# One decoder layer on one core: the sample softmax's last group in smaller pieces, prompt attention begun on half the tokens, three mixers moved behind the last attention unit

## The chip, the cores and the metric

The kernel runs on one core of a Trainium2 chip. The metric is the device time in microseconds (us) of one execution, the median over runs. The core has a matrix engine (PE, with its own queue of weight loads, PEld), a vector engine (DVE), a scalar engine (ACT), a general engine (POOL) and a queue that issues DMAs (SP). Each engine runs its own instructions in order and waits for the others by semaphores.

## The reference

One layer of a decoder for a prompt of 1024 tokens and a sample group of 8 x 4 tokens, model width 1024. The part that the change touches is the attention half:

```python
u, v, cq, ckv, kpe = split_in(rms_norm(xp, g_mix[l]) @ w_in[l])
a_out, _ = chunk_gmlp(u, v, w_s[l], b_s[l], ln_v_g[l], ln_v_b[l])
ckv_n = rms_norm(ckv, g_kv_a[l])
q = mla_queries(cq, pos_p, g_q_a[l], w_uq[l], g_qk_q[l])
k, vv = mla_keys_values(ckv_n, kpe, pos_p, w_uk[l], w_uv[l], g_qk_k[l])
b_out = mla_prompt_attend(q, k, vv)
xp = xp + merge_out(a_out, b_out, g_out_a[l], g_out_b[l], w_o[l])
```

There are 8 heads; q and k have 64 columns without and 32 with rotation, and are normalised per head and token; attention is causal. merge_out normalises both halves per token and multiplies by one matrix. The sample tokens do the same, except that each of the 8 sequences attends to 32 pages of 128 cached tokens (latents of 256, from which k is made per head) and to itself. Behind that come an attention to 256 memory tokens and a gated feed-forward with a convolution of width 3, which the change does not touch.

## The kernel before

A float32 product is three matmuls of rounded halves (`mm3`, L185): high by high, low by high, high by low. A tensor's split into halves is a cast on ACT (L191) and a difference on DVE or POOL (L192).

**Start of prompt attention** (`phase2a`, from L600). Tokens come in tiles of 128, in groups of two tiles: four groups of the prompt, and one of the 32 sample tokens. `proj_group` makes a list of parts for one group: per tile a q part and a k part (product on PE, copy and squares on ACT, a reduction on DVE), then six norm steps, mostly small DVE instructions (sums of squares to a reciprocal root, L222 to L236, then the scaling of k on DVE, L848, and POOL, L849), and, in a second list, one value part per tile (six matmuls, a copy on ACT). For heads 0 to 3 all five groups are done whole, group by group, before attention. `head_prep` then transposes, for one head, k of tiles 0 to 3, k of 4 to 7, q of 0 to 3, q of 4 to 7 (L872), and splits the results. Up to here a list scheduler orders the instructions of each engine.

**Prompt attention** is ordered by hand on PE, ACT, DVE and POOL (SP stays with the list scheduler). A unit is one head and two query tiles 2G and 2G+1; 32 units. It has scores (`a`, on PE, with a reduction to the row maximum `nm` on DVE, L903, L899, L905), an exponential (`e`, ACT, L909), and G+1 steps, each with transposes of the weights (`T`, L918, copied to `pth` by ACT, L920) and products with the values (`V`, L930); `out` divides by the sum (L935, L936) into `b_all`. The scores of a unit are put two units ahead of its steps. There are 80 steps t; lists `extra[t]` carry the preparation of the other heads.

**Mixers.** `mix_steps` normalises two finished tiles of attention output: squares on ACT (L1490), a root of eleven small DVE instructions, scaling on ACT (L1496), eight transposes on PE (L1501), copies on DVE to `hl`, and a DMA to memory (L1505). Three of them run in the last steps of prompt attention, each begun as soon as its last head is out.

**Sample attention** (`phase2b`): 8 batches of 16 steps, ordered by hand. A step makes the scores of one pair of pages (24 x 3 matmuls with k made on the fly, squares on ACT, reductions on DVE, L1278) and, from four steps behind the batch's last on, the value products of the batch before (L1348). `batch_softmax` is cut into parts, put at (step, position) by a table in `phase2b`; its last group of 64 columns per token is rooted, scaled and reduced to a maximum on DVE (r = 5 and 6), the maximum is transposed (r = 7, L1326), spread by a product with ones (r = 9, L1334) and subtracted on POOL (L1337), and the exponential follows on ACT (r = 10).

## Time and profile before

| what | us |
|---|---|
| runs | 1875.66, 1881.53, 1884.12 |
| median of the runs | 1881.53 |
| profiled execution | 1887.48 |
| its span, from the first to the last instruction | 1885.8 |
| prompt attention ordered by hand, about | 221.4 to 434.7 |
| sample attention, one batch | 57.3 |

A row of the order of time gives the start, the duration, the engine, the line of the code, the operation, what is written and read, the shape, and how many like instructions are in the row; in brackets stands the idle time ahead of it and what ended it. A row of waits names the waiting engine's instruction and the one waited for, then the us in total, the number of waits and the longest. The mean granted clock of the PE over the execution is 0.985 of full; in the windows a clock of 0.50 means that the matrix engine ran at half speed there.

### The profile page before, as it was taken

The numbers are of one execution on the slowest core, as the hardware profiler recorded it, in microseconds if no ns is written. First come the engines' busy times: TensorE is split into PE (matmuls) and PEld (weight loads), VectorE is DVE, ScalarE is ACT, GpSimd is POOL, SyncE is SP. The second block draws the span as 40 slices with busy tenths as digits, with TensorE's granted clock in tenths as the row PEclk, the third lists the DMA queues.
The fourth block names the chain that finished last, engine by engine and source line by source line (L and its number), as shares of the span: only waits on it lengthen the run. The fifth ranks groups of instructions, "written<-read, shape, count | busy, mean of one in ns | idle before, by whom it ended". The sixth has DMA issues, their size and how long they took to land.

```text
span 1885.8 us, 39848 instructions
## 1 busy us (share of the span) xinstructions
PE 1822.9 (97%) x14402; PEld 1757.2 (93%) x14402; DVE 1380.2 (73%) x2883; ACT 927.5 (49%) x1965; POOL 715.1 (38%) x826
## 2 busy tenths in 40 slices
PE   6999899989999999999999999999999999999999
PEld 6999799889999999998799988999999999999999
DVE  6865967766777667776654676788888888879664
ACT  6435676666555555555443355633332333344442
POOL 1221515643544455444213100157677677500000
PEclk9999899999999999999999999999999999999999
DMA  8102204666765665664564335322222222395252
GB/s 294 60 10 69 80 1 163 228 223 186 213 196 167 187 179 169 175 170 148 171 177 134 134 134 163 128 80 69 91 69 94 77 69 80 99 363 164 79 153 76
DMA packets 135559, 260.18 MB, mean 138 GB/s; under 512 B 20417, under 2 KB 78626, under 8 KB 132290
## 3 DMA queue, kind: packets, MB, share of 16 engines
q1 hardware_dynamic: 134498, 256.58, 43.4%
q8 instruction: 114, 1.87, 0.4%
q10 hardware_dynamic: 864, 1.05, 0.2%
q14 instruction: 83, 0.68, 0.1%
HBM read 212.27 MB, written 45.30 MB: 137 GB/s over the span
## 4 chain that ended last, share of the span: by engine, by line
PE 60%; DVE 6%; issue 4%; DMA 3%; POOL 2%; SPq 1%; ACT 1%; POOLq 0%; DVEq 0%; ACTq 0%
PE d L185 12%; PE s L185 11%; PE b L185 7%; PE F L185 7%; PE X L185 6%; PE E L185 6%; PE A L185 3%; PE y L185 3%; DMA cT<-cT 1%; PE o L1348 1%; DVE mx L1299 1%; POOL S L1296 1%; PE t L185 1%; PE v L185 1%; SPq L1207 1%
## 5 line engine op out<-in xcount | busy, mean ns | idle before, releaser
L185 PE MATMUL s<-w2h,ch 128*128 128x288 f32 (+1 forms) x1024 | 303.8, 297 | 0.0
L185 PE MATMUL s<-w2h,cl 128*128 128x288 f32 (+1 forms) x1024 | 295.1, 288 | 2.7 <-POOL cl L1235 1.4
L185 PE MATMUL s<-w2l,ch 128*128 128x288 f32 (+1 forms) x1024 | 294.7, 288 | 0.0
L185 PEld LDWEIGHTS s<-w2h,ch 128*128 128x128 f32 x1024 | 192.6, 188 | 10.8 <-issue 8.3
L185 PEld LDWEIGHTS s<-w2h,cl 128*128 128x128 f32 x1024 | 192.4, 188 | 3.4 <-POOL cl L1235 1.9
L185 PEld LDWEIGHTS s<-w2l,ch 128*128 128x128 f32 x1024 | 192.8, 188 | 0.0
L1278 DVE TENSOR_REDUCE ss<-sq 128x16 f32<-128x1024 f32 x128 | 155.6, 1215 | 49.3 <-ACT sq L1275 48.4
L1235 POOL TENSOR_TENSOR cl<-cT,ch 128x512 fp32r<-128x512 f32 x64 | 83.7, 1307 | 160.7 <-ACT ch L1231 128.9
L1275 ACT ACTIVATE sq<-s 128x512 f32<-128x512 f32 x128 | 76.5, 598 | 90.0 <-PE s L185 90.0
L1272 ACT ACTIVATE sq<-s 128x512 f32<-128x512 f32 x128 | 76.8, 600 | 78.0 <-PE s L185 78.0
L191 ACT CAST a<-brb 128x528 fp32r<-128x528 f32 x77 | 48.8, 634 | 111.0 <-PE d L185 107.1
L185 PE MATMUL mm<-whi,xh 128*128 128x256 f32 (+3 forms) x288 | 84.5, 294 | 14.4 <-ACT xh L195 9.8
L185 PE MATMUL d<-a,w 128*128 128x264 f32 x768 | 95.4, 284 | 1.0 <-DVE G L2064 1.0
L192 DVE TENSOR_TENSOR a<-brb,a 128x528 fp32r<-128x528 f32 x77 | 54.4, 707 | 57.2 <-ACT a L191 57.1
L185 PEld LDWEIGHTS d<-a,w 128*128 128x128 f32 x768 | 94.3, 188 | 1.1 <-issue 1.1
L185 PE MATMUL mm<-wlo,xh 128*128 128x256 f32 (+3 forms) x288 | 83.3, 292 | 0.0
L185 PE MATMUL mm<-whi,xl 128*128 128x256 f32 (+3 forms) x288 | 83.2, 293 | 0.0
L930 PEld LDWEIGHTS o<-v,pth 128*128 128x128 f32 x576 | 75.9, 197 | 7.3 <-ACT pth L920 5.2
L930 PE MATMUL o<-v,pth 128*128 128x64 f32 x576 | 76.2, 274 | 4.8 <-ACT pth L920 4.4
L1935 POOL TENSOR_TENSOR lo<-s,hi 128x1024 fp32r<-128x1024 f32 x20 | 63.0, 3148 | 45.7 <-ACT hi L1934 45.7
L1231 ACT CAST ch<-cT 128x512 fp32r<-128x512 f32 x128 | 73.5, 627 | 3.9 <-DMA cT<-cT 3.9
L1990 ACT COPY a<-A 128x264 f32<-128x264 f32 x43 | 16.1, 375 | 118.7 <-PE A L185 114.9
(714 smaller groups left out, 6472.2 us busy)
## 6 DMA issues: line engine op xcount, KB each, us to landing
cT<-cT SPq DMA_DIRECT2D x256, 160.0 KB, 2.5
ck<-ck SPq DMA_DIRECT2D x256, 144.0 KB, 3.4
raw<-w_up SPq DMA_DIRECT2D x44, 512.0 KB, 3.6
wsumd<-wsum SPq DMA_DIRECT2D x13, 1024.0 KB, 4.3
actd<-cv SPq DMA_DIRECT2D x44, 264.0 KB, 2.6
brb<-actd SPq DMA_DIRECT2D x44, 264.0 KB, 5.9
wsum<-w_down SPq DMA_DIRECT2D x11, 1024.0 KB, 5.2
raw<-wsumd SPq DMA_DIRECT2D x20, 512.0 KB, 3.8
```

Source lines behind the costliest of these rows:

```text
L185: self.nc.tensor.matmul(out, l, r, start=first and i == 0, stop=last and i == len(seq) - 1)
L191: {"act": nc.scalar.copy, "pool": nc.gpsimd.tensor_copy, "dve": nc.vector.tensor_copy}[eng](hi, src)
L192: low = lambda: nc.vector.tensor_tensor(lo, src, hi, ALU.subtract)
L930: nc.tensor.matmul(u["o"][:, e], th[:, z * P : z * P + P], s["v"][:, jj, h % 4], start=j == z == 0, stop=e == 1 and jj == 2 * G + 1)
L1207: nc.sync.dma_start(ck[j * 32 : j * 32 + 32], I["ck"][bass.ds(rv, 1)].rearrange("a t s f -> (a t) s f"))
L1231: nc.scalar.copy(d["h"][:, k], src[k])
L1235: (nc.vector if k else nc.gpsimd).tensor_tensor(d["l"][:, k], src[k], d["h"][:, k], ALU.subtract)
L1272: nc.scalar.activation(sq[:, 0], ps[:, :, n0 : n0 + 256], AF.Square)
L1275: nc.scalar.activation(sq[:, 1], pt.rearrange("p (e d) -> p e d", e=2), AF.Square)
L1278: yield lambda: nc.vector.tensor_reduce(s["ss"][:, g0 : g0 + 2].rearrange("p e (z h) -> p z e h", z=2), sq.rearrange("p z e (h d) -> p z e ...
L1296: e.tensor_tensor(x, x, ss[:, g0:g1].rearrange("p g h -> p (g h)").unsqueeze(2).broadcast_to([P, n, 4]), ALU.mult)
L1935: eng.tensor_tensor(lo, src, hi, ALU.subtract)
```

## The change

Three edits, and the changes of shape that they bring:

- **Softmax.** The last group's parts are cut smaller and put later: the first root step at step 16, the rest of the root in two pieces in step 17, scaling and maximum in step 18, transpose in step 19 (before: 18), product with ones in 20 (19), exponential in 21 (20). The output of a batch moves one step on as well. The last batch has its parts in a list that runs after the steps, in the order as before.
- **Mixers.** The three mixers wait in a list `ready` and are begun one per step from step 72 on, behind the step's other work. They scale in place and no longer copy into "k" tiles; the squares and the transposed result use "q" and "k" tiles instead of a "v" tile. Each tile's result has a DMA of its own, 256 KB instead of 512 KB for two. The transposed result is held per tile, so copies write one contiguous piece.
- **Start of prompt attention.** Before attention only the q and k parts of tiles 0 to 7, the norms of groups 0 and 1, and the transposes of k and q of tiles 0 to 3 for head 0 are done. Units 0 and 1 begin on these. In step 0 follow the norms of groups 2 and 3 interleaved, the eight value parts, the q and k parts of the sample group, and the transposes of tiles 4 to 7. The norm steps of the sample group are spread over steps 4 to 9, head 1's transposes start at step 1 instead of 0, and a table `ahead` puts the scores of units 2 to 4 behind the transposes that they need.

```diff
@@ -485,7 +485,8 @@
         self.close("pg")
         def mix(i0):
-            hl = self.t(pl, [P, 4, 256], F32, "hl")
+            hl = self.t(pl, [P, 2, 4, P], F32, "hl")
+            hl = [hl[:, i] for i in range(2)]
             self.mix_group(pl, pp, 0, i0, min(i0 + 2, 9), lambda i: a_all[:, i], hl, lambda j: self.t(pl, [P, 512], F32, "csq", 4), ("st", 3))
@@ -642,15 +643,20 @@
         rq = self.t(p, [P, 8, 8], F32, "rq")
...
         groups = ((0, 2), (2, 4), (4, 6), (6, 8), (8, 9))
-        for g in groups:
-            for f in sum(self.proj_group(p, pp, 0, *g, st[0], c, ("mm", 5)), []):
+        gs = [self.proj_group(p, pp, 0, *g, st[0], c, ("mm", 5)) for g in groups[:4]]
+        for g in range(2):
+            for f in gs[g][0]:
+                f()
+        for g in range(2, 4):
+            for f in gs[g][0][:-6]:
                 f()
...
         pm = self.open("p2m")
-        for f in self.head_prep(pm, pp, 0, st[0], c):
-            f()
+        prep = self.head_prep(pm, pp, 0, st[0], c)
+        for i in (0, 2):
+            prep[i]()
         st.append({**heads(), **self.proj_weights((pm, [P, 512], F32, "pth", 5), 1)})
@@ -660,13 +666,19 @@
             for j, f in enumerate(fs):
...
 
+        extra[0] += [f for fs in zip(*(gs[g][0][-6:] for g in range(2, 4))) for f in fs]
+        for g in groups[:4]:
+            extra[0] += self.proj_group(p, pp, 0, *g, st[0], c)[1]
+        sample = self.proj_group(p, pp, 0, 8, 9, st[0], c)[0]
+        extra[0] += sample[:-6] + [prep[1], prep[3]]
+        spread(sample[-6:], 4, 10)
         for h in (1, 2, 3, 5, 6, 7):
...
             else:
-                spread(fs, max(0, 10 * h - 16), 10 * h - 8 if h > 1 else 3)
+                spread(fs, max(1, 10 * h - 16), 10 * h - 8 if h > 1 else 4)
         late = [self.proj_group(p, pp, 1, *g, st[1], c) for g in groups]
@@ -691,26 +703,21 @@
                 yield from self.sample_prep(pp)
...
 
-            hls = []
-
-            def mix(G):
+            def mix(G, ring):
                 yield
-                if not hls:
-                    hl = self.t(p, [P, 8, 4, 64], F32, "v", 2).rearrange("p a b c -> p (a b c)")
-                    hls.extend(hl[:, a : a + 1024].rearrange("p (k n) -> p k n", k=4) for a in (1024, 0))
-                hl = hls.pop()
-                nt = lambda j: self.t(p, [P, 2, 4, 96], F32, "k", 4).rearrange("p m h d -> p (m h d)")[:, :512]
-                for k, _ in enumerate(self.mix_steps(pm, pp, 1, 2 * G, 2 * G + 2, lambda i: self.b_all[G][:, i % 2], hl, nt, ("tp", 4))):
-                    yield
-                    if k:
-                        yield
-
-            mixes = {28: 0, 29: 2, 30: 1}
+                hl = [self.t(p, [P, 2, 4, 96], F32, ring, 4).rearrange("p m h d -> p (m h d)")[:, :512] for _ in range(2)]
+                hl = [x.rearrange("p (k n) -> p k n", k=4) for x in hl]
+                yield from self.mix_steps(pm, pp, 1, 2 * G, 2 * G + 2, lambda i: self.b_all[G][:, i % 2], hl, None, ("tp", 4))
+
+            mixes, ready = {28: (0, "q"), 29: (2, "q"), 30: (1, "k")}, []
             wsums = dict(zip(range(22, 75, 4), (NK, NK + 1, *range(NK))))
...
             for n, u in enumerate(units):
-                nu = units[n + 2] if n + 2 < len(units) else None
                 k = u["n"]
+                if n < 3:
+                    ahead = ((), ((2, 0, 0), (2, 1, 0)), ((3, 0, 0), (3, 1, 1), (4, 0, 2), (4, 1, 2)))[n]
+                else:
+                    ahead = [(n + 2, e, e * k // 2) for e in range(2)] if n + 2 < len(units) else ()
                 for j in range(k):
@@ -718,16 +725,15 @@
                         f()
...
                         if done in mixes:
-                            steps.append(mix(mixes[done]))
+                            ready.append(mixes[done])
                     outs = []
...
                     pend = []
-                    if nu:
-                        for e in range(2):
-                            if (e * k) // 2 == j:
-                                nu["a"](e)
-                                pend.append(lambda nu=nu, e=e: nu["e"](e))
+                    for m, e, at in ahead:
+                        if at == j:
+                            units[m]["a"](e)
+                            pend.append(lambda nu=units[m], e=e: nu["e"](e))
                     self.flush()
@@ -739,6 +745,8 @@
                     t += 1
...
                         steps.append(sample())
+                    if t >= 72 and ready:
+                        steps.append(mix(*ready.pop(0)))
                     steps = [x for x in steps if next(x, 0) is None]
@@ -1071,7 +1079,8 @@
                 f()
 
-        hl = self.t(p, [P, 4, 288], F32, "ck", 15).rearrange("p k n -> p (k n)")[:, :1024].rearrange("p (k n) -> p k n", k=4)
+        hl = self.t(p, [P, 4, 288], F32, "ck", 15).rearrange("p k n -> p (k n)")[:, :1024].rearrange("p (m k n) -> p m k n", m=2, k=4)
+        hl = [hl[:, i] for i in range(2)]
         mix = self.mix_steps(pa, ppt, 1, 6, 8, lambda i: self.b_last[:, i % 2], hl, None, ("m", 1))
@@ -1079,7 +1088,7 @@
             n = b * 16
...
             at(n - 8, 2, lambda b: self.batch_enter(st[b], b), b)
-            for r, (k, pos) in enumerate(((12, 0), (13, 0), (14, 0), (14, 3), (15, 0), (16, 0), (16, 2), (18, 0), (18, 3), (19, 2), (20, 2))):
+            for r, (k, pos) in enumerate(((12, 0), (13, 0), (14, 0), (14, 3), (15, 0), (16, 0), (17, 0), (17, 3), (18, 2), (19, 2), (20, 0), (20, 2), (21, 3))):
                 f = lambda b=b, r=r: self.batch_softmax(p, ppt, st[b], r, b == NB - 1)
@@ -1091,7 +1100,7 @@
                 lambda b=b: self.batch_out(pt, st[b], 1, ppt),
...
             )
-            for k, pos, f in ((0, 3, tail[0]), (1, 2, tail[1]), (3, 3, tail[2])):
+            for k, pos, f in ((0, 3, tail[0]), (2, 2, tail[1]), (4, 3, tail[2])):
                 if b < NB - 1:
@@ -1314,22 +1323,24 @@
         elif r == 5:
...
             next(s["it"])
+        elif r == 6:
             next(s["it"])
-        elif r == 6:
+        elif r == 7:
             for _ in s["it"]:
                 pass
+        elif r == 8:
             scale(nc.vector, 24, 32)
...
             nc.vector.tensor_tensor(s["m"][:, 0], s["m"][:, 0], s["m"][:, 1], ALU.max)
-        elif r == 7:
+        elif r == 9:
             tp = s["tp"] = self.t(pp, [P, 512], F32, "m", 1)
             nc.tensor.transpose(tp[:32, :P], s["m"][:, 0], self.ident)
-        elif r == 8:
+        elif r == 10:
             mm = self.t(p, [32, 1], F32, "mm", 2)
...
             nc.vector.tensor_scalar(s["dg"], self.ident[:32, :32], mm, None, ALU.mult)
-        elif r == 9:
+        elif r == 11:
             bc = self.t(pp, [P, 512], F32, "m", 1)[:, :32]
@@ -1486,11 +1497,10 @@
 
...
             ns.append(n)
-            o = n if nt else hl[:, 2 * (i - i0) : 2 * (i - i0) + 2].rearrange("p k n -> p (k n)")[:tn]
+            o = n if nt else hl[i - i0][:tn].rearrange("p k n -> p (k n)")
             nc.scalar.activation(o, src(i)[:tn], AF.Square, accum_out=r[:, i - i0 : i - i0 + 1])
...
         self.rsqrt(p, r, r, 1.0 / 512)
-        w = m * tn
         yield
@@ -1499,10 +1509,11 @@
             tp = self.t(pp, [P, 512], F32, *tt).rearrange("p (k n) -> p k n", k=4)[:, :, :tn]
...
                 nc.tensor.transpose(tp[:, k], n[:, k * P : k * P + P], self.ident[:tn, :tn])
-            nc.vector.tensor_copy(hl[:, :, i * tn : i * tn + tn], tp)
+            nc.vector.tensor_copy(hl[i][:, :, :tn], tp)
+            o = t0 + i * tn
+            nc.sync.dma_start(self.mix_dram[:, z * 4 : z * 4 + 4, o : o + tn], hl[i][:, :, :tn])
             if nt is None and i < m - 1:
                 yield
-        nc.sync.dma_start(self.mix_dram[:, z * 4 : z * 4 + 4, t0 : t0 + w], hl[:, :, :w])
 
     def mixed(self):
```

Line numbers move by 8 to 11 in the changed code. PE at the start of prompt attention, before (k_2451 and k_2545 are groups 0 and 1, k_2639 and k_2733 groups 2 and 3; s are scores, prs the weights of units 0 and 1):

```order
L872 MATMUL tp_2887<-ident_60,k_2451 96x128 x2
L872 MATMUL tp_2887<-ident_60,k_2545 96x128 x2
L872 MATMUL tp_2894<-ident_60,k_2639 96x128 x2
L872 MATMUL tp_2903<-ident_60,q_2452 96x128 x2
...
L872 MATMUL tp_2894<-ident_60,k_2733 96x128 x2
L185 MATMUL s_2976<-kTh_2885,qTh_2901 128x128
...
L918 MATMUL tp_3010<-ident_60,prs_477_2974 128x128
L918 MATMUL tp_3010<-ident_60,prs_480_2982 128x128 x2
L185 MATMUL s_3018<-kTh_2885,qTh_2910 128x320
```


PE at the same place, now (k_2455 and k_2533 are groups 0 and 1, k_2611 group 2; wv are the value parts, the rows of 32 the sample group):

```order
L880 MATMUL tp_2722<-ident_60,k_2455 96x128 x2
...
L880 MATMUL tp_2731<-ident_60,q_2456 96x128 x2
...
L185 MATMUL s_2795<-kTh_2720,qTh_2729 128x128
...
L926 MATMUL tp_2829<-ident_60,prs_442_2793 128x128
L926 MATMUL tp_2829<-ident_60,prs_445_2801 128x128 x2
L185 MATMUL tp_2889<-wvh_1725,ckh_1700 128x256
L185 MATMUL tp_2889<-wvl_1726,ckh_1700 128x256
...
L185 MATMUL tp_2954<-wqh_1715,cqh_1698 32x384
...
L880 MATMUL tp_2977<-ident_60,k_2611 96x128 x2
...
L880 MATMUL tp_2985<-ident_60,q_2612 96x128 x2
...
L926 MATMUL tp_2993<-ident_60,prs_448_2811 128x128
...
L185 MATMUL s_3002<-kTh_2720,qTh_2983 128x320
```


The value parts and the sample's parts, which stood before all transposes, now stand between the first transposed weights and the transposes of groups 2 and 3. DVE at the end of prompt attention, before (pr and nm with s_5490 and s_5495 are one query tile of the last unit, with s_5537 and s_5542 the other; mixr is a mixer's sum of squares):

```order
L899 ISA nm_5489 128x1
L905 TENSOR_SCALAR nm_5489<-nm_5489,rq_2449 128x1
L222 TENSOR_SCALAR rqx_1071_5511<-mixr_5476 128x2
L223 TENSOR_SCALAR rqy_1073_5513<-rqx_1071_5511 128x2
...
L235 SCALAR_TENSOR_TENSOR rqh_1072_5512<-rqa_1074_5514 128x2
L236 SCALAR_TENSOR_TENSOR mixr_5476<-rqh_1072_5512,rqy_1073_5513 128x2
L935 RECIPROCAL rsum_2968<-rsum_2968 128x2
L936 TENSOR_TENSOR b_all_2400<-o_5459,rsum_2968 128x2x64
L903 TENSOR_SCALAR pr_1077_5535,nm_5536<-s_5537 128x512
L899 ISA pr_1077_5535,nm_5536<-s_5542,cmask_2424,nm_5536 128x512
...
L905 TENSOR_SCALAR nm_5536<-nm_5536,rq_2449 128x1
```


DVE there, now (nm_5487 and nm_5519 are the two query tiles):

```order
L913 TENSOR_SCALAR nm_5487<-nm_5487,rq_2453 128x1
L943 RECIPROCAL rsum_2787<-rsum_2787 128x2
L944 TENSOR_TENSOR b_all_2404<-o_5463,rsum_2787 128x2x64
L911 TENSOR_SCALAR pr_1069_5518,nm_5519<-s_5520 128x512
L907 ISA pr_1069_5518,nm_5519<-s_5525,cmask_2428,nm_5519 128x512
...
L913 TENSOR_SCALAR nm_5519<-nm_5519,rq_2453 128x1
L943 RECIPROCAL rsum_2788<-rsum_2788 128x2
L944 TENSOR_TENSOR b_all_2404<-o_5531,rsum_2788 128x2x64
L222 TENSOR_SCALAR rqx_1082_5566<-mixr_5549 128x2
L223 TENSOR_SCALAR rqy_1084_5568<-rqx_1082_5566 128x2
...
L236 SCALAR_TENSOR_TENSOR mixr_5549<-rqh_1083_5567,rqy_1084_5568 128x2
```


The mixer's root, eleven rows, moved from between the two query tiles of the last unit to behind both. DVE at the softmax of the first batch's last group, before (ss are the sums to be rooted, mx the maxima; S_7441 and ss_7442 belong to the next batch's scores):

```order
L1289 TENSOR_TENSOR ss_6369<-ss_6369,kss_6370 128x64
L222 TENSOR_SCALAR rqx_1393_8124<-ss_6369 128x64
...
L236 SCALAR_TENSOR_TENSOR rqy_1395_8126<-rqh_1394_8125,rqy_1395_8126 128x64
...
L231 SCALAR_TENSOR_TENSOR rqa_1396_8127<-rqy_1395_8126 128x64
...
L236 SCALAR_TENSOR_TENSOR ss_6369<-rqh_1394_8125,rqy_1395_8126 128x64
L1296 TENSOR_TENSOR S_6368<-S_6368,ss_6369 128x256
L1299 TENSOR_REDUCE mx_8024<-S_6368 128x32
L1323 TENSOR_TENSOR mx_8024<-mx_8024 128x32
L1235 TENSOR_TENSOR cl_8136<-cT_7832,ch_8135 128x512
L1278 TENSOR_REDUCE ss_7442<-sq_8165 128x2x2x4
```


DVE there, now (S_7447 and ss_7448 belong to the next batch's scores):

```order
L1298 TENSOR_TENSOR ss_6374<-ss_6374,kss_6375 128x64
L222 TENSOR_SCALAR rqx_1391_8130<-ss_6374 128x64
...
L1244 TENSOR_TENSOR cl_8138<-cT_7838,ch_8137 128x512
L1287 TENSOR_REDUCE ss_7448<-sq_8167 128x2x2x4
...
L236 SCALAR_TENSOR_TENSOR rqy_1393_8132<-rqh_1392_8131,rqy_1393_8132 128x64
...
L231 SCALAR_TENSOR_TENSOR rqa_1394_8133<-rqy_1393_8132 128x64
...
L1287 TENSOR_REDUCE ss_7448<-sq_8214 128x2x2x4
...
L1305 TENSOR_TENSOR S_6373<-S_6373,ss_6374 128x256
L1308 TENSOR_REDUCE mx_8030<-S_6373 128x32
L1334 TENSOR_TENSOR mx_8030<-mx_8030 128x32
L1244 TENSOR_TENSOR cl_8272<-cT_7976,ch_8271 128x512
L1287 TENSOR_REDUCE ss_7448<-sq_8301 128x2x2x4
```


The last group's root, scaling and maximum stood close behind each other; now the work of the next batch's first two steps stands between their pieces. On PE the transpose of the maximum moved 50 rows on, behind the matmuls of two more half steps.

## The prediction

> **What bounds the kernel now.** I read the page's first part, then the waits of the PE, then the windows around the three places that the diff touches, then the order of time inside them.
>
> ```profile
> span 1885.8 us, 39848 instructions
> PE 1822.9 (97%) x14402; PEld 1757.2 (93%) x14402; DVE 1380.2 (73%) x2883; ACT 927.5 (49%) x1965; POOL 715.1 (38%) x826
> ```
>
> The PE (matrix engine) is busy for 97% of the span, and the change removes no matmul. So it can only win or lose time in which the PE stands still, or runs at a lower granted clock. The waits of the PE say where it stands (releaser: us in total, times, longest):
>
> ```profile
> PE m L1326 <- DVE mx L1323: 6.3, 7, 0.9
> PE o L930 <- ACT pth L920: 4.4, 1, 4.4
> PE tp L872 <- DVE rqa L234: 2.3, 1, 2.3
> PE s L1250 <- POOL krq L1222: 1.7, 2, 1.3
> PE tp L872 <- DVE wvl L192: 1.5, 1, 1.5
> PE s L185 <- POOL cl L1235: 1.4, 1, 1.4
> PE s L185 <- DVE cl L1235: 1.3, 1, 1.3
> ```
>
> The first is the sample softmax (edit A), the second the end of prompt attention (edit B), the third and fifth its start (edit C), the fourth and the last two the beginning of the sample stage behind it. The windows (length, then busy us of PE, PEld, DVE, ACT, POOL, granted clock, DMA share, GB/s):
>
> ```profile
> 196.00:209.40 13.40, 11.32 (x77) 10.18 (x76) 13.02 (x47) 9.83 (x54) 10.29 (x23) 1.00 0.23 64
> 209.40:216.50 7.10, 5.05 (x38) 4.11 (x36) 6.72 (x25) 6.74 (x38) 4.78 (x8) 1.00 0.90 317
> 216.50:226.70 10.20, 7.38 (x26) 5.87 (x27) 9.63 (x47) 4.56 (x12) 1.13 (x1) 0.50 0.01 4
> 226.70:233.60 6.90, 6.90 (x29) 6.45 (x28) 4.91 (x16) 2.59 (x7) 1.46 (x4) 0.50 0.01 2
> 233.60:250.00 16.40, 16.40 (x138) 15.91 (x136) 10.12 (x34) 13.12 (x28) 0.00 (x0) 1.00 0.00 1
> 408.00:421.20 13.20, 8.54 (x66) 7.75 (x64) 7.17 (x29) 9.82 (x22) 7.59 (x9) 1.00 0.58 222
> 421.20:428.10 6.90, 6.88 (x34) 6.89 (x34) 4.65 (x23) 3.63 (x9) 0.00 (x0) 0.51 0.31 109
> 510.80:568.20 57.40, 56.50 (x478) 53.16 (x477) 42.07 (x82) 32.40 (x71) 28.42 (x48) 1.00 0.69 195
> ```
>
> Two of these places pay twice. Behind each stretch of idling the clock is granted at a half: 17.1 us at the start of attention, 6.9 us at the end. The PE has no gap in the last 6.9 us of each, so each loses half of 6.9, that is 3.4 us, which stands in no wait. In the sample stage (one batch: 57.4 us) the PE misses 0.9 us and no other engine comes near it.
>
> **Edit A: the last softmax group.** Seven batches have this chain, in order of time:
>
> ```profile
> 548.46 1.12 DVE L1289 TENSOR_TENSOR ss<-ss,kss 128x64 f32<-128x64 f32 x1
> 554.23 0.19 DVE L1323 TENSOR_TENSOR mx<-mx 128x32 f32<-128x32 f32 x1
> 554.40 0.69 DVE L1235 TENSOR_TENSOR cl<-cT,ch 128x512 fp32r<-128x512 f32 x1
> 554.47 0.28 PE L1326 MATMUL m<-ident,mx 128*32 128x128 f32 x1 [0.90 <-DVE mx L1323]
> 555.01 1.22 DVE L1278 TENSOR_REDUCE ss<-sq 128x16 f32<-128x1024 f32 x1
> 560.96 0.40 PE L1334 MATMUL m<-dg,ones 32*128 32x32 f32 x2
> 561.82 2.47 POOL L1337 TENSOR_TENSOR S<-S,bc 128x1056 f32<-128x1056 f32 x1 [1.12 <-ACT bc L1336]
> ```
>
> DVE runs root, scaling and maximum from 548.46 to 554.42 in one piece, and the PE reaches the transpose 0.9 us early. After the change the transpose stands in step 19, position 2, where before the product with ones stood: the PE gets there at 560.96 less the 0.9 it no longer waited, 560.1. DVE lets the work of two steps pass between the pieces: one cl (0.69), two reductions (1.22 each) and small additions, 3.5 us in all. The maximum is ready at 554.4+3.5 = 557.9, some 2.1 us ahead of the PE. All that follows (product with ones, POOL's 2.47 us subtraction, the exp) moves on by one step, a sixteenth of 57.4, 3.6 us. The value products begin four steps behind the batch's last step; the exp in step 21, position 3 lies two steps ahead of the first product that needs the new weights. So this costs nothing; if that cover failed, the price would be POOL's 2.47 us in each of 7 batches, 17.3 us (rival 5). Gain: 7 x 0.9 = **6.3**; bounds 0 (a new wait as long) and 6.3.
>
> **Edit B: the mixers behind the last unit.** Before:
>
> ```profile
> 411.51 0.16 DVE L222 TENSOR_SCALAR rqx<-mixr 128x2 f32<-128x2 f32 x1
> 414.48 0.16 DVE L236 SCALAR_TENSOR_TENSOR mixr<-rqh,rqy 128x2 f32<-128x2 f32 x1
> 416.66 0.21 DVE L905 TENSOR_SCALAR nm<-nm,rq 128x1 f32<-128x1 f32 x1
> 416.91 1.24 ACT L909 ACTIVATE pr<-pr,nm,rq 128x1024 f32<-128x1024 f32 x1 [2.27 <-DVE nm L905]
> 418.15 1.32 ACT L1496 ACTIVATE k<-b_all,mixr 128x512 f32<-128x512 f32 x2
> 419.99 0.61 ACT L1490 ACTIVATE k<-b_all 128x512 f32<-128x512 f32 x1
> 420.60 1.04 ACT L920 COPY pth<-tp 128x512 f32<-128x512 f32 x2
> 437.17 8.36 SPq L1207 DMA_DIRECT2D ck<-ck  x12
> 437.24 0.40 PE L185 MATMUL s<-w2h,cl 128*128 128x288 f32 x1 [1.26 <-DVE cl L1235]
> 453.75 0.49 PE L1250 MATMUL s<-bd,krq 128*128 128x128 f32 x2 [1.33 <-POOL krq L1222]
> ```
>
> A mixer's eleven root instructions (411.51 to 414.64, 3.1 us of DVE) stand ahead of the last unit's reductions. That delays nm, hence ACT's exp, hence the copy pth at 420.60 that the PE waits 4.4 us for; two scalings (1.32) and two squares (0.61 each) stand between as well. The change puts the roots behind nm and the squares behind the exp. Then nm comes 2.8 us earlier (scores done at about 412.7, two reductions and nm about 1.2: 413.9 instead of 416.7), the exp ends at 415.9, two squares at 417.1, and the copy ends at about 417.6. The PE waits there 1.3 instead of 4.4: −3.1. Two later mixers now have their squares in front of a copy in the same way; about 1.3 of ACT each, partly covered: +0.6 and +1.1. The half clock of 421.2 to 428.1 had the 4.4 us wait and the 65% busy window before it; without that wait I take it as gone: −3.4. The first pages' two waits for cl (1.4 and 1.3) shrink by 1.0 together, since POOL and DVE have these pieces ready while the PE still transposes. Sum **−5.8** by 437.24.
>
> The new DMAs: six of 256 KB for three of 512 KB on SP's queue, the same bytes. The last of them must issue before the page loads at 437.17; it moves forward with the PE or more, and the wait at 453.75 (1.33), for the pages behind it, ends somewhere between kept and gone: take half, **−0.7**. Bounds of B: everything, −7.1; if the half clock comes all the same, −6.5 + 3.4 = −3.1; if besides the two later copies are each late by a full 1.3 and the pages gain nothing, −3.1 + 2.6 − 1.0 = −1.5.
>
> **Edit C: attention on half the tokens.**
>
> ```profile
> 208.81 0.68 DVE L848 TENSOR_TENSOR k<-k,hr 128x512 f32<-128x512 f32 x1
> 220.19 0.69 DVE L848 TENSOR_TENSOR k<-k,hr 128x512 f32<-128x512 f32 x1
> 204.82 0.28 PE L185 MATMUL mm<-wvh,ckh 128*128 128x256 f32 x1
> 204.93 0.28 PE L185 MATMUL mm<-wvl,ckh 128*128 128x256 f32 x1
> 221.72 0.46 PE L185 MATMUL s<-kTh,qTh 96*128 96x128 f32 x1
> 226.85 0.61 PE L185 MATMUL s<-kTh,qTh 96*128 96x320 f32 x1
> ```
>
> The k of tokens 0 to 511 is scaled at 208.81, that of the last group at 220.19; the first score waits for the later one. After the change the first transposes need only the earlier: the DVE chain to it (13.02 busy of 13.4) is not shortened, so they start at about 209.5 and the first score at 211.5, ten us earlier. But the ten us are not gained, for the next units need the other half. I compare at 226.85, the first score on it. DVE is done with the first four score tiles at about 216, and has then the roots of groups 2 and 3: 28 instructions of about 0.2, two rq and two k of 0.68, together 7.3: k ready at 223.4. The PE has by then the eight value parts (48 matmuls) and the sample's two parts (12), 60 x 0.12 (the distance of the two wv rows) = 7.2 us, from about 216.9 to 224.1: both arrive together. Transposes, the split on ACT and DVE: the score of 226.85 comes at about 226.5. Up to there nothing is gained: the same DVE work lies on the path.
>
> What is at stake is the clock. If the dense 7.2 us bring it back to full, the 3.4 lost between 226.7 and 233.6 return. Against this, the PE loses those 7.2 us of filling from 196 to 216, where it is idle 2.1 of 13.4 already; idle grows to some 6 before 209.4, so the half clock may start there, and the first half of the value parts (6.8 us long, 3.4 worth) is then done at a half. That pushes the score to about 229.5, against an equivalent 230.25 (226.85 + 3.4) before: **−1** (rounded from −0.8). Bounds: −4 (clock full from the scores on) and +4 (all 7.2 us and what follows at a half: 216.9 + 14.4 + 2.4 = 233.7 less 230.25).
>
> [...]
>
> **Sum.** −6.3 − 5.8 − 0.7 − 1.0 = −13.8. Other edits (smaller hl tiles, copies of 512, a few list-scheduled rows in the output projection and memory attention that change places) lie behind a busy PE and I put them at 0, ±1. The profiled execution took 1887.5 (span 1885.8 plus 1.7 around it), so it would take 1873.7. The median of the three runs, 1881.5, is 6 lower; by the same difference it becomes **1867.7**.
>
> **Rivals.**
> 1. *The clock takes most of it back.* A holds, but the half clock stays at both ends of attention: B −3.1, C 0 to +2: sum −7.4 to −9.4, 1872 to 1874. For it: in the windows above each stretch of waits has such a tail, and 408.0 to 421.2 at 65% busy was enough for one. Against it: B's longest wait shrinks from 4.4 to 1.3. Chance 0.22.
> 2. *Short waits leave the clock alone.* Only the long stretches (4.4 us at 416.8; the 17.1 us of attention's start) call the half clock, and dense work ends it at once: B −6.5, C −4, A −6.3: −17, 1864.5. For it: the 0.9 us waits of the softmax, and 196.0 to 209.4 with 2.1 idle, keep 1.00. Against it: the fall at 216.5 behind waits of 1.5. Chance 0.14.
> 3. *Starved start, slower.* The half clock begins at about 200 and piecework keeps the PE starved under it: roots of 0.2 us between score reductions on DVE, value parts and scores each waiting for the next. At a half, every us of full-clock PE work costs one more. Before, 3.4 to 7 us were lost so; to come out 9.4 slower than before, against A and B's −12.8, 22 us more must be lost, so that the half clock reaches some 44 us of dense work on from 227, to about 270. At 24 us lost: 1881.5 − 12.8 + 24 = 1892.7. For it: the DVE's 13.02 of 13.4, with which the PE cannot be fed early. Against it: from 233.6 on the PE has no gap and DVE is busy 62%. Chance 0.11.
> 4. *The change does not do what it says* at one place: the PE waits for mx in the new position, or the squares delay the copy again: A or B alone, −7, 1874.5 to 1877. For it: the margin of 2.1 rests on my walk of DVE. Against it: DVE is busy 42 of 57.4, and the order of instructions shows that the pieces moved. Chance 0.06.
> 5. *The later softmax is late for the values*: 17.3 of A's chain appear as new waits: −13.8 + 17.3 = +3.5, 1885. Against it: two steps of 3.6 between exp and its first product. Chance 0.05.
>
> Main case: 0.42. Faster by more than 0.5% (9.4 us, about what a measurement here tells from no change) means below 1872.1: the main case nearly whole (0.41), rival 2 (0.14) and a third of rival 1 (0.07): 0.62. Slower: rival 3, 0.11. Within: the rest, 0.27. Range: the main case alone with its bounds (C −4 to +4, B −1.5 to −7.1) is 1861 to 1875; rivals 1, 2 and 4 lie in or just above it, and the other end takes in a kept wait or a lost C: 1860 to 1882.
>
> **What would show it.** Right: no wait of m on mx; 2a's last value product at about 430 less what C gives, with waits of 1.3 or less and clock 1.00 in 415 to 430; first score at 211 to 212, the score on the second half at 226 to 230. Wrong: a wait of m of any size in the new place; a window at 0.5 behind the last unit; clock 0.5 from 200 to past 235.

## The result

The change made the kernel a little slower: 1886.48 us (median of 21 runs, 1877.47 to 1889.15) against 1882.02 (median of 21 runs of the kernel before), ratio 1.0017, 95% interval 1.0007 to 1.0028, that is +3.2 us (+1.3 to +5.3). The two medians lie 4.5 us apart; the ratio, which has an interval, is what is used below. A second measurement on another chip gave 1.0018 (1.0006 to 1.0030). Forecast were 1867.7 us and a gain of 13.8. By the forecast's own bound of 0.5% this is "no change", but it lies above the stated range of 1860 to 1882.

The profiled executions are almost alike, 1886.88 now and 1887.48 before: that execution of the kernel before was one of its slower ones, 5 us above its median. The first rows of the page after:

```profile
span 1885.2 us, 39848 instructions
PE 1824.5 (97%) x14402; PEld 1756.9 (93%) x14402; DVE 1382.3 (73%) x2883; ACT 929.7 (49%) x1965; POOL 713.4 (38%) x826
```

PE's waits after the change (waiting instruction, releaser, us in total, times, longest):

```profile
PE s L185 <- POOL cl L1244: 4.7, 9, 1.6
PE mm L185 <- ACT ckh L191: 4.6, 1, 4.6
...
PE o L938 <- ACT pth L928: 2.0, 3, 1.3
PE s L185 <- ACT qTh L195: 2.0, 2, 1.2
PE tp L880 <- ACT hsq L831: 1.8, 1, 1.8
PE tp L1511 <- ACT b_all L1506: 1.7, 1, 1.7
```

The waits that the forecast wanted gone are gone or smaller: the seven of m on mx (6.3), the 4.4 on pth (now 2.0 in three pieces), the 2.3 on rqa. One that it wanted smaller, for POOL's cl (1.4 before, at 491.8), is not: 1.6, at 491.2. New ones have come: on POOL's cl (4.7 in nine, with that one), on ckh (4.6), on qTh, hsq and b_all. The windows around the three edits (length, then busy us of PE, PEld, DVE, ACT, POOL, granted clock, DMA share, GB/s):

```profile
202.30:209.40 7.10, 3.08 (x12) 3.09 (x13) 6.89 (x20) 2.82 (x14) 5.75 (x13) 0.79 0.29 77
209.40:217.30 7.90, 4.96 (x28) 3.83 (x28) 4.67 (x14) 5.12 (x26) 4.41 (x9) 0.93 0.91 317
217.30:230.70 13.40, 11.79 (x80) 10.40 (x79) 10.99 (x43) 9.55 (x30) 1.75 (x2) 0.88 0.02 6
230.70:237.50 6.80, 6.80 (x31) 6.50 (x30) 3.47 (x12) 1.27 (x3) 0.00 (x0) 0.52 0.01 2
421.90:432.00 10.10, 8.02 (x39) 7.43 (x38) 7.64 (x35) 6.66 (x13) 1.10 (x3) 0.51 0.42 153
567.00:624.10 57.10, 56.84 (x478) 53.27 (x477) 41.81 (x80) 32.09 (x71) 27.60 (x44) 1.00 0.61 176
```

The half clock at the end of attention lasts some 10 us instead of 6.9, at the start there is still one of 6.8 us without a gap in PE's work, and a batch takes 57.1 where 56.5 was forecast.

To see where the time went, the same PE instructions are set side by side in the traces. From the first q part of prompt attention to the third score of unit 3 (185.46 and 244.10 before) it takes 58.6 us in the profiled execution before, and 62.7 after. The eight heads end (the first product of the sample stage) at +1.97, as that product began at 434.85 before and 436.82 now; the first steps of the sample stage win 2.8 up to 467.6, so that the changed kernel leads by 0.8; a batch takes 57.07 instead of 57.41 (four batches from 612.10 to 841.74 before, 609.80 to 838.09 after), so that at 841.7 it leads by 3.65. That lead is lost between 890 and 1041, where the order of instructions is almost the same: the half clock there adds up to 20.5 us instead of 17.0, which is worth 1.7, and one wait for ACT (n, L1542 before) is 2.7 instead of 1.4.

### The profile page after: what moved, and what is told of

It reads as the page before. It is cut to its first block, busy times and chain, and to the rows that moved or that the text cites. A ratio compares the mean times of both kernels' runs of the same rounds, so it can differ in the third digit from the quotient of the medians.

```text
span 1885.2 us, 39848 instructions
## 1 busy us (share of the span) xinstructions
PE 1824.5 (97%) x14402; PEld 1756.9 (93%) x14402; DVE 1382.3 (73%) x2883; ACT 929.7 (49%) x1965; POOL 713.4 (38%) x826
## 4 chain that ended last, share of the span: by engine, by line
PE 75%; DVE 8%; DMA 5%; issue 5%; ACT 3%; SPq 2%; POOL 1%; DVEq 0%; POOLq 0%; ACTq 0%
PE s L185 13%; PE d L185 12%; PE mm L185 8%; PE b L185 7%; PE F L185 7%; PE X L185 6%; PE E L185 6%; PE A L185 3%; PE y L185 3%; PE o L938 2%; DMA cT<-cT 2%; PE tp L926 1%; SPq L1212 1%; PE tp L185 1%; PE o L1359 1%
```

## The experiments

All ratios are to the kernel before, on the same chip in the same rounds. A ratio of 0.001 is 1.9 us.

| kernel | what it has | median | ratio | 95% interval |
|---|---|---|---|---|
| a_only | softmax | 1880.22 | 0.9986 | 0.9972 to 1.0000 |
| a_fix | softmax, subtraction behind cl | 1877.76 | 0.9971 | 0.9959 to 0.9982 |
| b_only | mixers and shapes | 1881.10 | 0.9989 | 0.9977 to 1.0001 |
| c_only | start | 1892.14 | 1.0039 | 1.0025 to 1.0054 |
| c_shape | start and shapes | 1892.83 | 1.0057 | 1.0043 to 1.0072 |
| c_val | start, values ahead | 1892.14 | 1.0059 | 1.0039 to 1.0079 |
| c_late | start, sample parts in step 2 | 1887.60 | 1.0030 | 1.0017 to 1.0042 |
| v_late | values and sample parts late, no split | 1888.43 | 1.0034 | 1.0021 to 1.0046 |
| sums_early | sums of weights four steps earlier | 1883.68 | 1.0007 | 0.9995 to 1.0018 |
| ab_plain | softmax and mixers | 1877.20 | 0.9970 | 0.9958 to 0.9982 |
| ab_fix | a_fix and mixers | 1875.72 | 0.9960 | 0.9945 to 0.9975 |
| ab_spread | ab_fix, transposes one step later | 1875.72 | 0.9964 | 0.9952 to 0.9976 |
| bc | mixers and start | 1888.18 | 1.0026 | 1.0014 to 1.0038 |
| full_again | the whole change | 1886.26 | 1.0018 | 1.0006 to 1.0030 |
| full_fix | the whole change, with a_fix | 1877.53 | 0.9976 | 0.9963 to 0.9988 |

**a_only**: the three pieces of the diff in `phase2b`'s table, its tails and `batch_softmax`.

> The softmax table of the change alone, all else as before. Theory 1 (a new wait took the place of the old): the waits of m on mx are gone (7 x 0.9), but POOL's subtraction of 2.45 us now stands right ahead of its next cl, and PE waits for cl once per batch; the period of a batch falls by 0.35 us only (57.43 to 57.07), -2.4 us over seven batches, about -0.1%. Rival (the wait for cl in the changed kernel came from the other two edits, the softmax alone gives the forecast 6.3): period 56.5, -0.3%, no wait on cl of POOL in the steady batches.

The period of a batch is 57.09 (609.88 to 838.22 in four), and the waits on mx are gone; theory 1 holds. POOL's part of it, where a_only subtracts (start, duration, engine, line, operation, in brackets the idle time before and what ended it):

```profile
564.26 2.45 POOL L1339 TENSOR_TENSOR S<-S,bc 128x1056 f32<-128x1056 f32 x1 [7.09 <-ACT bc L1338]
566.67 1.28 POOL L1235 TENSOR_TENSOR cl<-cT,ch 128x512 fp32r<-128x512 f32 x1
...
568.01 0.41 PE L185 MATMUL s<-w2h,cl 128*128 128x288 f32 x1 [0.27 <-POOL cl L1235]
```

POOL was idle for 7 us, then subtracts for 2.45, and only then makes the cl that PE needs next. In the kernel before, a cl stands behind the subtraction (561.82) too, but it is ready at 565.53 and PE comes for it at 566.13:

```profile
564.23 1.30 POOL L1235 TENSOR_TENSOR cl<-cT,ch 128x512 fp32r<-128x512 f32 x1
...
566.13 0.29 PE L185 MATMUL s<-w2h,cl 128*128 128x288 f32 x1
```

What changed is PE's own work in between. Before, sixteen value products (561.29, 1.07 us) stand behind the product with ones; in a_only they stand ahead of it (559.18), so that PE comes for the cl 1.0 us sooner and finds it 0.4 late. The wait has 0.27 in the view of waits; the starts of the first two rounds of matmuls in that step lie 1.01 us apart (567.24 and 568.25) instead of 0.49 (565.78 and 566.27), so it costs 0.5.

**a_fix**:

```diff
-(17, 0), (17, 3), (18, 2), (19, 2), (20, 0), (20, 2), (21, 3)
+(17, 0), (17, 3), (18, 2), (19, 2), (20, 0), (21, 0), (22, 0)
```

> As a_only, but the product with ones and POOL's subtraction one half step later, behind POOL's cl of that step (step 21, position 0 instead of 20, position 2), and the exp at step 22, position 0 instead of 21, position 3. Theory 1: the wait for cl goes as well, the period falls to about 56.5 to 56.6, -5 to -6 us, about -0.3%. Rival (PE cannot go below 57.0 per batch because something else, DVE or the DMAs of the pages, then sets the pace): the period stays at 57.0 to 57.1 and -2 us as in a_only, with a wait under another name.

The order on POOL in a batch of this kernel:

```profile
554.60 1.29 POOL L1235 TENSOR_TENSOR cl<-cT,ch 128x512 fp32r<-128x512 f32 x1 [4.30 <-ACT ch L1231]
557.40 2.46 POOL L1339 TENSOR_TENSOR S<-S,bc 128x1056 f32<-128x1056 f32 x1 [1.50 <-ACT bc L1338]
559.82 0.46 POOL L1220 TENSOR_TENSOR krq<-cT,cosT 128x128 f32<-128x128 f32 x1
```

cl goes first, and the period is 56.52 (602.49 to 828.57): 0.89 less than before, the whole of the forecast 0.9. Theory 1 holds, the rival falls; neither DVE nor the pages set the pace at 57.0.

**b_only**: the diff's `mix`, `mixes`, `ready`, `mix_steps`, with the shapes.

> The mixers behind the last unit alone (with the smaller tiles and a DMA per tile). Theory 1: the wait of 4.4 us for pth falls to about 1.3, a wait of about 1.7 for the mixer's scaling appears, and the half clock behind them lasts as long as before or one window of 3.4 us longer, so that the sample stage begins within 1 us of before; the pages come earlier and the first steps of the sample stage give 2 to 3 us; then some of it is lost between 880 and 1060. In all -3 to +1 us. Rival (the half clock of 10.5 us in the changed kernel was an accident of the window's phase, which the earlier start moved): the half clock is 6.9 us or less here and the sample stage begins 3 to 6 us earlier, in all -4 to -8.

PE's waits from 400 to 440 in it, and the windows ahead of the half clock and of it:

```profile
PE o L925 <- ACT pth L915: 1.9, 3, 1.3
PE tp L1496 <- ACT b_all L1491: 0.8, 1, 0.8
PE s L185 <- POOL cl L1231: 0.8, 1, 0.8
```

```profile
408.00:417.00 9.00, 7.42 (x59) 6.69 (x58) 5.46 (x23) 6.82 (x16) 6.44 (x8) 1.00 0.51 213
417.00:424.00 7.00, 5.80 (x28) 5.27 (x27) 5.36 (x26) 6.08 (x12) 0.00 (x0) 0.51 0.23 77
```

The waits are as in the forecast (1.3, then small ones), but the half clock is there for 6.8 us. It is not an accident of this execution: in the eight profiles with the moved mixers it lasts 6.8 to 10.3 us at this place. By the time, -2.1 us (-4.3 to +0.2), theory 1 holds and the rival is at its edge. The marks in the trace don't decide: the half clock is no longer than before, and the sample stage begins 5.1 us earlier counted from the first q part, as the rival said; but in a_fix, which has the mixers as before, it begins 6.0 us earlier, so this mark says more of the execution of before than of the mixers.

**c_only**: the diff's hunks on `gs`, `prep`, `extra[0]`, `sample`, `spread` and `ahead`.

> The start of prompt attention alone. Theory 1 (it costs): the score that stood at 226.85 comes at about 229, a half clock of 7 us follows at 230 as before, and from unit 3 on everything lies 4 to 5 us later: +3 to +5 us against before, clear of zero. Rival (the later start in the changed kernel is the phase of the clock's windows only): the offset at unit 3 is 0 to 1.5, and the time is within 1.5 us of before.

+7.3 us (4.7 to 10.2), more than theory 1 said. In its trace the stretch from the first q part to unit 3 takes 59.6 us, where the seven other kernels that start as before (a_only, a_fix, b_only, ab_fix, ab_plain, ab_spread, sums_early) take 56.0 to 56.6 and only the profiled execution of before 58.6. So 3 us lie at the start: PE is idle there for 8.9 us, against 7.3 to 8.4 in the seven, and busy for 50.7 with the same products, against 47.8 to 49.3. Its half clock stands at 203.5 to 206.9 and 210.3 to 217.1, ahead of the score on the second half; behind this score c_only has none. Of the remainder I can show a part, at the end of attention. There the four additions of the last sum of weights on POOL fall on a mixer's root (POOL's rows, then DVE's, in order of time):

```profile
410.90 1.28 POOL L784 TENSOR_TENSOR wsum<-wsum 128x512 f32<-128x512 f32 x1
412.26 1.28 POOL L785 TENSOR_TENSOR wsum<-wsum 128x512 f32<-128x512 f32 x1
413.61 1.26 POOL L786 TENSOR_TENSOR wsum<-wsum 128x512 f32<-128x512 f32 x1
```

```profile
411.09 1.12 DVE L224 TENSOR_SCALAR rqy<-rqy 128x2 int32<-128x2 int32 x1
412.24 0.16 DVE L233 TENSOR_TENSOR rqa<-rqy 128x2 f32<-128x2 f32 x1
412.43 1.12 DVE L234 TENSOR_TENSOR rqa<-rqa,rqx 128x2 f32<-128x2 f32 x1
413.59 0.16 DVE L235 SCALAR_TENSOR_TENSOR rqh<-rqa 128x2 f32<-128x2 f32 x1
413.78 1.11 DVE L236 SCALAR_TENSOR_TENSOR rqy<-rqh,rqy 128x2 f32<-128x2 f32 x1
```

Of these five instructions on two columns, two take 0.16 us and three 1.11 to 1.12. Each of the three ends 0.01 to 0.03 us behind one of POOL's additions: 411.09 + 1.12 is 412.21, where POOL's addition ends at 412.18; the next such pair ends at 413.55 and 413.54, the third at 414.89 and 414.87. What holds them so long the rows don't show. The root of eleven takes 6.4 us (to 416.30) where that of before took 3.1, and PE waits 3.5 for b_all and then 3.2 for pth (before: 4.4 for pth alone).

**c_shape**: c_only, with the smaller tiles and a DMA per tile.

> The start of attention and the smaller tiles with a DMA per tile, the mixers and the softmax as before. Theory 1 (the smaller tiles let the list scheduler put the scaling of the last latents, ckr, four rows later on DVE, which costs nothing where DVE's chain to the last k decides, but is on the path once attention begins on half the tokens): PE waits about 4.6 us for ckh instead of 1.9, the first score comes 3 us later than in c_only counted from the first q part, and the offset at unit 3 is that of the whole change, 3 us above c_only. Rival (the 3 us come from the moved mixers or the softmax): wait for ckh 1.9 and the offset of c_only.

In length theory 1 holds: the stretch to unit 3 takes 62.7 us, as in the four kernels that have the whole of it (after, full_again, full_fix 62.7, bc 62.8). The way there is only in part the one that it named. Counted from the first q part, the first score is 1.1 later than c_only's, not 3, and the first score on the second half 0.6 later; the other 2.5 come behind it, where a stretch that ran at a clock of 1.00 in c_only (7.8 us) now runs at 0.67 (10.3). All five traces with both start and shapes have this half clock. That the shapes call it isn't shown: c_only's trace is one execution, and the intervals of the two times overlap. PE's longest waits from 200 to 240 in it, and the same in c_only:

```profile
PE mm L185 <- ACT ckh L191: 4.6, 1, 4.6
PE s L185 <- ACT qTh L195: 1.9, 2, 1.2
PE tp L886 <- ACT hsq L837: 1.8, 1, 1.8
```

```profile
PE s L185 <- ACT qTh L195: 1.9, 2, 1.2
PE mm L185 <- ACT ckh L191: 1.9, 1, 1.9
PE tp L885 <- ACT hsq L836: 1.4, 1, 1.4
```

The list scheduler, which orders everything ahead of attention, puts the scaling of the last latents on DVE (ckr) at 204.35 instead of 202.07, which is 1.1 us later counted from the first q part. In b_only and ab_plain, which have the shapes without the start, ckr comes 18.5 us behind the first q part, in a_only, without the shapes, 18.8: there they move nothing.

**c_val**: the value parts ahead of attention again, group by group.

```diff
-            for f in gs[g][0]:
+            for f in gs[g][0] + gs[g][1]:
...
-            for f in gs[g][0][:-6]:
+            for f in gs[g][0][:-6] + gs[g][1]:
...
-        for g in groups[:4]:
-            extra[0] += self.proj_group(p, pp, 0, *g, st[0], c)[1]
```

> The start of attention alone as in c_only, but the eight value parts stay ahead of attention, group by group, as before; step 0 keeps the norms of groups 2 and 3, the sample's parts and the transposes. Theory 1 (the 48 value matmuls in step 0 are what costs, since PE lacks them as filling at 196 to 209 and pays for them later): the clock does not fall before the first score, the second half's first score comes about 4 to 5 us earlier than in c_only, and the time is within 1.5 us of before. Rival (the split itself costs: the roots of groups 2 and 3 stand behind four score reductions on DVE, and the ACT queue delays the splits of k and q): the time stays 4 us or more above before, with PE idle in step 0 while it waits for the roots.

Theory 1 falls: 1.0059, not less than c_only, and the second half's first score comes 2.3 us later than there, not 4 to 5 earlier. PE has its filling and a clock of 1.00 up to the first score, and then waits 4.9 us for the second half's k on DVE at once:

```profile
PE tp L883 <- DVE k L859: 5.3, 2, 4.9
```

**v_late**: the opposite, no split of the start, only the value and sample parts behind the first step.

```diff
+        for g in range(4):
+            for f in gs[g][0]:
+                f()
...
+            extra[0] += self.proj_group(p, pp, 0, *g, st[0], c)[1]
+        extra[0] += sample[:-6]
```

> The kernel before, with only the eight value parts and the sample's parts moved behind the first step's transposes; attention is not begun on half the tokens, all norms and transposes of head 0 stand ahead as before. Theory 1 (these parts are filling that PE has to do in any case; ahead of attention they hide under DVE's chain, behind it they stand on PE's path): +4 to +7 us against before, as much as c_only or more. Rival (moving them is free or a gain, since the clock is back sooner behind dense matmuls, and only the split of the start costs): within 2 us of before.

+6.4 us: theory 1. Both parts of the edit cost by themselves: what is taken from under DVE's chain comes back on PE's path, and what is split leaves a wait for DVE (4.9 us in c_val). They don't add: c_val (which still has the sample's parts in step 0) costs 11.1 us, v_late 6.4, and c_only, with both, 7.3.

**c_late**:

```diff
-        extra[0] += sample[:-6] + [prep[1], prep[3]]
+        extra[0] += [prep[1], prep[3]]
+        extra[2] += sample[:-6]
```

> The start of attention alone as in c_only, but the sample group's q and k parts (12 matmuls, six ACT copies and squares) come in step 2 instead of step 0. Theory 1 (of about 4 us that the start costs, the sample's parts on PE, 1.7, and their ACT work ahead of the splits of k and q, about 1.5, make up the greater part): the first score on the second half comes 2 to 3 us earlier than in c_only, and the time lies 2 to 3 us below c_only, about +5 against before. Rival (k of groups 2 and 3 is the limit there, ready on DVE only at 225.8): the score comes less than 1 us earlier, and the time is that of c_only.

The second half's first score comes 2.2 us earlier than in c_only, counted from the first q part, as theory 1 said. But step 2 pays it back: up to unit 3 it takes 60.2 us against 59.6. The time (+5.7) lies below c_only's within the intervals of both. Inconclusive on the time; the place is no gain.

**sums_early**:

```diff
-            wsums = dict(zip(range(22, 75, 4), (NK, NK + 1, *range(NK))))
+            wsums = dict(zip(range(18, 71, 4), (NK, NK + 1, *range(NK))))
```

> The kernel before, with the fourteen sums of weights on POOL each four steps of attention earlier, so that the last one (four additions of 1.28 us) no longer falls on the mixers' roots at the end of attention. Theory 1 (POOL's two-operand additions stretch the roots' two-operand DVE instructions from 0.16 to 1.12 us, 3 to 6 us for one root, and the waits of 4.4 or 3.5 and 3.2 us at the end of attention come from that as much as from the order): the root of eleven takes about 2.0 us, the waits at the end of attention fall to 2.5 us or less, and the time is 2 to 5 us below before. Rival (the order alone makes the wait; the additions do not matter, or do the same harm where they now are): waits of 4 us or more stay and the time is within 1.5 us of before.

The rival holds: the disturbed root takes 2.7 us, the wait for pth stays at 4.4, the time is that of before. c_only's rows don't show that the length hangs on two operands: L224, which reads one tile, takes 1.12 us too. The order makes the wait; that the additions make the end of attention worse where a whole root meets them rests on c_only's rows alone.

**ab_fix**, a_fix and b_only together:

> The change without its start of attention, and with the subtraction behind POOL's cl (a_fix and b_only together). Theory 1 (the edits are separate and add): ratio 0.9971 x 0.9989 = 0.9960, -7.5 us against before; period of a batch 56.5, no wait of m on mx, no wait for cl in the steady batches. Rival (the gain of the mixers was the luck of the clock's windows in that kernel's runs, or is eaten by a softmax that now meets the pages earlier): -5.4 or less, as a_fix alone.

0.9960: the product of the two, to the digit. This is the best version, with ab_spread: 0.4% faster than the kernel before and, by the two ratios (0.9960/1.0017), 0.6% faster than the change.

**ab_spread**: in `mix`, one more step behind the scaling (`if k == 2: yield`).

> ab_fix with one step of attention more between a mixer's scaling on ACT and its transposes on PE. Theory 1 (the half clock at the end of attention stays because the remaining waits of 1.3 for pth and 1.8 for the scaled tile are enough for it): the wait of 1.8 goes, the 1.3 stays, and a half clock of at least 3.4 us stays; the time is within 2 us of ab_fix, ratio to before 0.995 to 0.997. Rival (the one wait of 1.8 keeps the clock down): no half clock between 415 and 435, 3 to 5 us less than ab_fix, ratio 0.993 to 0.9945.

Theory 1 by the time, which is ab_fix's: the wait for the scaled tile is gone and the half clock stays, for 10.2 us. But those for pth grow to 4.3 in three (longest 2.7), so the kernel doesn't show what the one wait of 1.8 is worth.

**full_fix**:

> The whole change with the subtraction behind POOL's cl. Theory 1 (the edits add, the start costs 7 us here too): 0.996 x 1.0039 = 0.9999, within 2 us of before and 6 to 8 us above ab_fix. Rival (the start's cost in c_only came from the end of attention, where the sums of weights fell on the mixers' roots, which the moved mixers avoid): 2 to 4 us above ab_fix, ratio about 0.998.

0.9976, 3 us above ab_fix: nearer to the rival. As the whole change had measured 1.0017, three more kernels were set side by side on one chip: **full_again**, **ab_plain** (the change without its start) and **bc** (without its softmax).

> The whole change as it is, beside the next two on one chip. Theory 1 (the edits add; the start of attention costs about 3 us where the mixers are moved, since half of the 7.3 of c_only lay at the end of attention): -2.9 - 2.1 + 3 = -2, ratio 0.999; the 1.0017 of the first measurement was in part that chip's runs. Rival (the start costs 7 us in the whole change too, in places that the trace of one execution does not show): +2.5 us, ratio 1.0013 to 1.002.

> The change without its start of attention, the softmax as the change has it. Theory 1: -2.9 - 2.1 = -5, ratio 0.9973, 3 us below full_again and 2 to 3 us above ab_fix. Rival: 7 us below full_again.

> The change without the softmax: mixers and start of attention. Theory 1: -2.1 + 3 = +1, ratio 1.0005, with the waits of m on mx (0.9 in each of seven batches) and no wait of 3 us for b_all at the end of attention. Rival: -2.1 + 7.3 = +5, ratio 1.0028.

Rival in all three: the start costs 9.0 us in the whole change (1.0018 against 0.9970) and 7 beside the mixers (1.0026 against b_only's 0.9989, on another chip); by the intervals each is uncertain by about 3. The traces of full_again and ab_plain show where. Of the same PE instructions, full_again's stand 0.4 us later at the first q part, 6.7 at unit 3, 5.0 at the first product of the sample stage, 5.5 to 5.7 from there to 883, and 7.8 at 1041. In the last stretch the half clock adds up to 20.5 us in the one and 17.0 in the other, which is worth 1.7, and the wait for ACT's n is 2.7 instead of 0.6; the trace doesn't say which of them counts. That full_fix came out only 3 us above ab_fix (with an uncertainty of about 4) stays open. Its trace has +6.5 up to unit 3 too; from there to the sample stage ab_fix's trace takes 191.6 us where b_only, ab_plain and ab_spread, with the same code there, take 187.7 to 189.7, and full_fix 187.5.

## Why the prediction was wrong, step by step

**Reading.** That PE's waits and the half clock behind them are all that can be won, and where they stand, was right, but for one wait: the 1.4 for POOL's cl was counted with the first pages behind attention and stands 57 us behind their start. The first two edits add (0.9971 x 0.9989 = 0.9960); with the start they needn't (full_fix 0.9976, the product 0.9999). One sum is wrong: with its bounds the main case reaches from 1864 to 1878, not from 1861 to 1875; the stated range holds both. What failed is three terms: A gave 3.7 less than forecast, B 4.4 less, and C cost 10.0 more in the whole change, 18.1 together, where 17.0 are to be explained.

**Edit A**, forecast -6.3, measured -2.6 (a_only; 0 to -5.3), by the period -0.32 a batch. The walk of DVE was right: mx was in time, and so was the exp. The step that failed is the sentence that the moved subtraction "costs nothing": I looked at who needs its result, two steps on, and not at the cl behind it on POOL. That cl stood behind it before as well, with 0.6 us to spare; one step on it comes 0.4 late. a_fix puts the cl first and gives the forecast gain: 6.2 by the period, 5.5 by the time.

**Edit B**, forecast -6.5, measured -2.1 (-4.3 to +0.2). The waits came as computed, 1.3 first and, in the whole change, 1.7 for the scaled tile in place of 1.1. The term that failed is the half clock: "without that wait I take it as gone" was my assumption, and no run bears it out. It stayed in all eight profiles with the moved mixers, 6.8 to 10.3 us, against 3.4 to 13.6 in those without. With its 3.4 struck out, the step's own bound of -3.1 lies in the measured interval. In b_only the clock was at 0.51 from 417.0 to 424.0, behind 9.0 us in which it was 1.00 and PE was busy for 7.42, with no single wait above 1.3.

**Edit C**, forecast -1 between -4 and +4, measured +7.3 alone and 9.0 in the whole. Its score on the second half came at 229.55 as forecast (229.5), but that is luck, as three errors cancel. The value parts began at 218.02 instead of 216.9. They and the sample's parts took 8.5 us, where 7.2 and 3.4 of half clock were reckoned: only the first ten value products ran at a half (0.21 apart up to 220.09, then 0.12). And 3.1 us passed from there to the score instead of 2.4.

The first score was 2.8 us late against 211.5, which was worked out from DVE's chain alone. Of this 0.7 is there at the first q part already. About 1.0 is there in c_only too: the splits of k and q stand on ACT behind the squares of the other half's parts (in the whole change kTh at 212.62). The last 1.1 comes with the shapes and the scheduler's choice, which I had put at 0, ±1.

Two steps failed and stay in the sum. One is what follows the score on the second half. Its 3.4 us of half clock were booked as returned and no wait was reckoned: 13.8 us from there to unit 3 (17.25 before, less 3.4). It took 19.3, with 6.8 at a half (230.7 to 237.5, in every trace with both start and shapes) and 1.5 of waiting; in c_only, without half clock there, 16.8 with 1.8 of waiting. The other is the comparison. In the profiled execution before the half clock ends 48.1 us behind the first q part (233.6 less 185.5), and 42 to 44 us behind it in the seven other kernels with that start: I compared with one execution, the one with the longest tail. The stretch to be beaten was 56.0 to 56.6, not 58.6. These two make up the 6.3 us that the start costs up to unit 3; the rest of the 9 stands in the later stretches listed above, and its cause isn't shown.

**Rivals.** The side was rival 3's, a start that costs more than A and B give; its mechanism was not, since the half clock ends at 237.5 and does not reach to 270. Rival 1 named the clock, rightly for B. None named a queue behind a moved instruction.

## What to carry to other kernels

When an instruction moves, look at what stands behind it on its engine and how soon that is needed, before asking who waits for its result: half a step in a table was worth 3 us here. Filling that hides under another engine's chain was free here, and cost nearly its whole length when it was put behind that chain (in v_late 6.4 us, for 60 matmuls that take 7.5 at the spacing seen at full clock, 0.12 us and, for the sample's q part, 0.17). Before counting a clock's recovery as a gain, compare several executions: one alone can hold a tail of several us that others don't have (here the half clock ended 48.1 us behind the first q part in the one, 42 to 44 in seven others).

## What the runs showed of the hardware

Up to 435 us, the half clock began at 39.0, 216.5, 312.1 and 421.3 in the profiled execution of before, and lasted 6.8, 17.1, 6.8 and 6.8 us; in that of the whole change it began at 39.2, 206.5, 216.7, 230.4 and 421.5, and lasted 6.8, 3.4, 3.4, 6.8 and 10.3 us. Behind one and the same wait of 2.08 us, of the same scores for a DVE piece (at 312.06 before), the clock was at a half for 6.8 us in before, for 3.4 in a_fix, and not at all in full_again, the whole change. The two windows behind that wait, of before and of full_again:

```profile
312.10:318.90 6.80, 6.80 (x29) 6.77 (x30) 3.23 (x11) 0.95 (x2) 6.43 (x6) 0.50 0.54 224
```

```profile
316.00:319.50 3.50, 3.50 (x26) 3.27 (x27) 2.48 (x9) 0.84 (x2) 3.39 (x3) 1.00 0.38 159
```

So behind this wait the clock cost 3.4 us in before (half of 6.8) and nothing in full_again; what makes the difference the traces don't show. The half clock also came behind a stretch in which PE stood still for less: in b_only PE was busy for 7.42 of the 9.0 us up to 417.0. And in c_only a root of small DVE instructions ran beside POOL's four additions: it took 6.4 us instead of 3.1, with 1.11 to 1.12 us for the three instructions that end within 0.03 us behind an addition, and 0.16 for the two between.
